# Where the first weights of a Strassen product begin in SBUF: 96 instead of 288 bytes behind a multiple of 512

## The chip, the cores and the metric

The kernel runs on one core of one Trainium2 chip. The metric is the device time of one execution in microseconds (us), as the median of the runs that were made; smaller is better. A profile is one further execution, recorded by the hardware profiler.

## What is computed

One residual block of a hybrid decoder over 512 positions of 1024 channels, in float32. Cut to its outline:

```
h = rmsnorm(x, norm1_g);  proj = h @ w_in
y_a = a_b * causal_dwconv(a_c * a_x)
y_b = native sparse attention (compressed, selected and windowed keys), 8 heads of 64
x = x + (sigmoid(gA) * (y_a @ w_a_out) + sigmoid(gB) * (y_b @ w_b_out)) @ w_o
h = rmsnorm(x, norm2_g);  gu = h @ w_ffn_in            # 1024 x 5632
g = causal_dwconv(gu[..., :2816], ffn_conv_w) + ffn_conv_b
x = x + (silu(g) * gu[..., 2816:]) @ w_ffn_out         # 2816 x 1024
```

The change lies in the product with `w_ffn_in`.

## The kernel before

Every float32 operand of a matmul is cut into a high part (rounded to the matmul's format) and a low part (the rest), and a product is three matmuls: high weights by high stream, high by low, low by high. The weights of a matmul are a 128x128 block (512 bytes in each partition) and the stream is what is multiplied by them, 512 or 256 columns wide.

The program has one queue of instructions per engine, whose order a scheduler fixed when the program was built. TensorE (PE) is busy from the first matmul to the last. The second half, from about 364 us, is the feed-forward part. `ff_strassen` goes over the 22 blocks of 128 hidden channels in 11 pairs, each once for the gate (n = 0) and once for the up weights (n = 1), so there are 22 calls of `ff_pair`. Each multiplies a 2x2 arrangement of weight blocks by a 2x2 arrangement of the stream with seven products in place of eight (Strassen's scheme in Winograd's form). The order of the products in `ff_pair` is a22, a11, a12, 2, 3, 4, 1. Each is a `dense` call: four steps along the contraction, each with high weights on the high and on the low stream (L405, L406), and then four with the low weights (L408). That is 12 matmuls of 256 columns a product and 84 a call. Between two calls `down_part` puts the product with `w_ffn_out`: matmuls of 512 columns that write `pdn`. The first call is written in another order (L969 and L975).

The names in the profile:

- `xf_h`, `xf_l`: high and low parts of the stream of all seven products; `ah`, `al`: the stream of `down_part`.
- `th`, `tl`: high and low parts of the weight block a22, written in `ff_forms`; two buffers each.
- `wh_s`, `wl_s`: parts of a11 and a12. `sh`, `sl`: parts of the four sums of blocks, by the names 1 to 4. `wh_d`, `wl_d`: parts of the weights of `down_part`.
- `gap_x`, `gap_w`: tiles that nobody writes or reads; they only move what is allocated after them.

A pool hands out addresses in the order in which the names of its tiles appear first. The pool `pw` begins directly behind `xf_l`. Line 832 names `th` there ahead of the gap, and everything else of the pool comes behind it. So the start addresses in a partition are, with the remainder on division by 512 (in this text: the phase):

| tile | starts at byte | phase |
| --- | --- | --- |
| `xf_h`, `xf_l` | 37152, 65824 | 288 |
| `th` (two buffers) | 94496, 96544 | 288 |
| `tl` (two buffers) | 98784, 100832 | 480 |
| sums, `sh`, `sl`, `p1` | 102880 to 135648 | 480 |
| `wh_s`, `wl_s`, `wh_d`, `wl_d` | from 204768 | 480 |
| `ah`, `al` | from 138720 | 480 |

Steps inside these tiles are multiples of 512 bytes, so each block of weights and each stretch of stream has the phase of its tile.

Of the kernel before, what the change touches and what calls it, by code (L numbers as in the profile page):

```python
# [11 lines left out]
F32 = mybir.dt.float32  # L12
# [6 lines left out]
P = 128  # L19
# [63 lines left out]
def tile_block(ctx: ExitStack, tc: tile.TileContext, xT, pos, par, par2, w_tok, w_a3, w_gate, w_ao, w_bo, w_o,  # L83
# [12 lines left out]
    def const(shape, name, dt=F32, pool=sb):  # L96
        return pool.tile(shape, dt, name=name, tag=name)
# [731 lines left out]
    xf_h = const([P, 4, 7, TH], "xf_h", F32R, px)  # L829
    xf_l = const([P, 4, 7, TH], "xf_l", F32R, px)  # L830
    pw = ctx.enter_context(tc.tile_pool(name="pw", bufs=1, side="left"))
    pw.tile([P, D // 2], F32R, name="th_", tag="th", bufs=2)
    const([P, 48], "gap_w", F32, pw)

    def x_forms(k, v):
        nc.vector.tensor_sub(v[:, T1:T3 + 1], v[:, 1:4:2], v[:, 0:2])
# [273 lines left out]
```

## Time and profile before

| what | value |
| --- | --- |
| median of 3 runs | 715.76 us (715.33 to 716.61) |
| the profiled execution | 715.21 us |
| its span, first to last instruction | 713.5 us |
| granted TensorE clock | 1.000 |

The span leaves out what the execution needs ahead of its first and behind its last instruction, 1.7 us here. In the listing by time a row is a run of like matmuls: its start, how long it lasted (the recorded end of the last one, and these overlap), the engine, the line, and what is written from what. A matmul's own recorded length is longer than the step from its start to the next start, since matmuls follow one another before they end; the step is what costs time, and it is read from the starts.

### The profile page before, as it was taken

To read this page: it belongs to the slowest core of one execution; us is meant where nothing else is said; L and a number is where in the kernel's file an instruction comes from. 1 tells how busy PE (TensorE), PEld (TensorE's weight loads), DVE (VectorE), ACT (ScalarE), POOL (GpSimd) and SP (SyncE) were. 2 spreads that over 40 slices of the span, in tenths; PEclk is the share of its full clock that TensorE was granted. 3 is DMA by queue.
4 is the path that set the end of the run, shared out by engine and by line. 5 is a ranking of instruction groups with operands and counts; after the bars stand their busy time and mean duration, and the time that the engine had idled before them with its cause. 6 is when DMAs were issued, how large, how long until landed. Compare 5 with 4: busy or idle time off the path is not lost.

```text
span 713.5 us, 11375 instructions
## 1 busy us (share of the span) xinstructions
PE 708.3 (99%) x4285; PEld 633.5 (89%) x4285; DVE 534.8 (75%) x957; ACT 432.6 (61%) x722; POOL 182.4 (26%) x179
## 2 busy tenths in 40 slices
PE   9999999999999999999999999999999999999997
PEld 9999878888888888888889999899999999999986
DVE  6887886687566878365795899988787877878643
ACT  7535655977667776522676767666555765647440
POOL 4051422133433334433012220221211222111110
PEclk9999999999999999999999999999999999999999
DMA  7333687511121122336386797987978779785565
GB/s 274 97 95 119 172 181 162 135 60 59 60 69 51 60 76 73 118 128 197 94 197 137 174 236 196 226 209 183 213 183 211 175 185 206 185 198 105 123 142 149
DMA packets 41142, 105.47 MB, mean 148 GB/s; under 512 B 3968, under 2 KB 9216, under 8 KB 41088
## 3 DMA queue, kind: packets, MB, share of 16 engines
q1 hardware_dynamic: 26528, 70.41, 30.4%
q0 software_dynamic: 14272, 34.08, 27.6%
q8 instruction: 33, 0.54, 0.3%
q10 hardware_dynamic: 288, 0.26, 0.1%
q14 instruction: 21, 0.17, 0.1%
HBM read 102.64 MB, written 2.10 MB: 147 GB/s over the span
## 4 chain that ended last, share of the span: by engine, by line
PE 96%; DMA 2%; ACT 1%; issue 0%; DVE 0%; POOL 0%; ACTq 0%; POOLq 0%
PE p L406 9%; PE p L405 9%; PE p L408 9%; PE pdn L406 6%; PE pdn L405 6%; PE pdn L408 6%; PE pg L406 4%; PE pg L405 4%; PE pg L408 4%; PE pa L405 2%; PE pt L681 2%; PE pa L406 2%; PE pa L408 2%; PE po L405 2%; PE po L406 2%; PE po L408 2%
## 5 line engine op out<-in xcount | busy, mean ns | idle before, releaser
L406 PE MATMUL p<-xf_l,sh 128*128 128x256 f32 x336 | 80.6, 277 | 0.0
L405 PE MATMUL p<-xf_h,sh 128*128 128x256 f32 x336 | 80.5, 277 | 0.0
L153 ACT ACTIVATE sh<-s 128x1024 fp32r<-128x1024 f32 x44 | 46.2, 1057 | 38.2 <-PE p L406 24.7
L406 PE MATMUL pdn<-al,wh_d 128*128 128x512 f32 x176 | 68.8, 391 | 0.0
L405 PE MATMUL pdn<-ah,wh_d 128*128 128x512 f32 x176 | 68.5, 390 | 0.0
L405 PEld LDWEIGHTS p<-xf_h,sh 128*128 128x128 f32 x336 | 63.0, 188 | 0.1
L406 PEld LDWEIGHTS p<-xf_l,sh 128*128 128x128 f32 x336 | 63.0, 188 | 0.1
L161 POOL DMA_DIRECT2D wl_s<-in_w_ff_dram x22 | 19.5, 885 | 167.2 <-ACT wl_s L160 155.9
L154 DVE TENSOR_TENSOR sl<-s,sh 128x1024 fp32r<-128x1024 f32 x44 | 53.8, 1224 | 8.7 <-ACT sh L153 8.7
L159 ACT ACTIVATE wh_s<-wr_s 128x1024 fp32r<-128x1024 f32 x22 | 23.3, 1059 | 53.1 <-PE pdn L406 50.1
L408 PE MATMUL p<-xf_h,sl 128*128 128x256 f32 x336 | 51.5, 277 | 0.0
L136 POOL TENSOR_TENSOR wl_g<-wr_g,wh_g 128x1024 fp32r<-128x1024 f32 x16 | 38.4, 2401 | 50.7 <-ACT wh_g L134 25.4
L405 PE MATMUL pg<-xg_h,wh_g 128*128 128x512 f32 x128 | 50.7, 396 | 0.0
L406 PE MATMUL pg<-xg_l,wh_g 128*128 128x512 f32 x128 | 50.6, 395 | 0.0
L408 PE MATMUL pdn<-ah,wl_d 128*128 128x512 f32 x176 | 47.7, 389 | 0.0
L161 POOL DMA_DIRECT2D wl_d<-in_w_dn_dram x22 | 26.5, 1203 | 77.2 <-ACT wl_d L160 69.0
L1029 DVE TENSOR_TENSOR x<-x,pdn 128x512 f32<-128x512 f32 x48 | 33.0, 688 | 16.2 <-PE pdn L408 15.5
L408 PEld LDWEIGHTS p<-xf_h,sl 128*128 128x128 f32 x336 | 44.6, 188 | 0.2
L405 PE MATMUL p<-xf_h,wh_s 128*128 128x256 f32 x168 | 40.5, 276 | 0.0
L406 PE MATMUL p<-xf_l,wh_s 128*128 128x256 f32 x168 | 40.5, 276 | 0.0
L408 PEld LDWEIGHTS pdn<-ah,wl_d 128*128 128x128 f32 x176 | 33.0, 188 | 6.9
L406 PEld LDWEIGHTS pdn<-al,wh_d 128*128 128x128 f32 x176 | 33.0, 188 | 6.2
(359 smaller groups left out, 2123.1 us busy)
## 6 DMA issues: line engine op xcount, KB each, us to landing
wr_s<-in_w_ff_dram SPq DMA_DIRECT2D x44, 512.0 KB, 4.9
wl_s<-in_w_ff_dram POOLq DMA_DIRECT2D x22, 512.0 KB, 7.2
wr_d<-in_w_dn_dram SPq DMA_DIRECT2D x22, 512.0 KB, 7.0
wl_d<-in_w_dn_dram POOLq DMA_DIRECT2D x22, 512.0 KB, 8.2
wr_g<-in_w_gate_dram SPq DMA_DIRECT2D x16, 512.0 KB, 3.4
wr_a<-in_w_a_dram SPq DMA_DIRECT2D x12, 512.0 KB, 4.1
tl<-in_w_ff_dram POOLq DMA_DIRECT2D x22, 256.0 KB, 6.9
wl_a<-in_w_a_dram POOLq DMA_DIRECT2D x10, 512.0 KB, 7.9
```

What stands on the lines that cost most here:

```text
L136: e.tensor_sub(lo[:, 0:n], raw[:, 0:n], hi[:, 0:n].bitcast(F32))
L153: hi = nc.scalar.activation(h, v, AF.Copy)
L154: nc.vector.tensor_sub(l, v, h.bitcast(F32))
L159: nc.scalar.activation(h, raw, AF.Copy)
L161: nc.gpsimd.dma_start(l if dst is None else dst, src, accum_op=ALU.add)
L405: nc.tensor.matmul(acc, wh, xh, start=first and i == 0, stop=False)
L406: nc.tensor.matmul(acc, wh, xl, start=False, stop=False)
L408: nc.tensor.matmul(acc, wl, xh, start=False, stop=last and i == len(units) - 1)
L681: nc.tensor.transpose(pt[:, i * P:(i + 1) * P], e[:, i, (kt + k0) * P:(kt + k0 + 1) * P], ident)
L1029: nc.vector.tensor_add(xj, xj, acc)
```

## The change

Two lines: a new gap of 320 bytes ahead of `th`, and a gap of 384 in place of 192 bytes behind it.

```diff
     pw = ctx.enter_context(tc.tile_pool(name="pw", bufs=1, side="left"))
+
+    const([P, 80], "gap_v", F32, pw)
     pw.tile([P, D // 2], F32R, name="th_", tag="th", bufs=2)
-    const([P, 48], "gap_w", F32, pw)
+    const([P, 96], "gap_w", F32, pw)
```

The start of `th` moves by 320 bytes, to 94816 and 96864, phase 96. `tl`, the sums, `sh`, `sl` and `p1` move by 320 + 192 = 512 bytes and keep phase 480. All else stays where it was. Every engine has the same instructions with the same waits in the same order as before.

## The prediction

> **What bounds the kernel now.** I read the page first: the line of busy times, then the chain that ended last.
>
> ```profile
> span 713.5 us, 11375 instructions
> PE 708.3 (99%) x4285; PEld 633.5 (89%) x4285; DVE 534.8 (75%) x957; ACT 432.6 (61%) x722; POOL 182.4 (26%) x179
> PE 96%; DMA 2%; ACT 1%; issue 0%; DVE 0%; POOL 0%; ACTq 0%; POOLq 0%
> ```
>
> PE is busy for 99% of the span and makes up 96% of the chain. In the feed-forward part, where the change lies, it has no idle time at all:
>
> ```profile
> core 0: us, PE busy (x) PEld busy (x) DVE busy (x) ACT busy (x) POOL busy (x), PEclk, DMA share, GB/s
> 477.60:687.90 210.30, 210.30 (x1513) 196.92 (x1512) 161.45 (x224) 123.56 (x164) 39.83 (x40) 1.00 0.77 178
> ```
>
> So the end of the kernel is set by how fast PE gets through its queue, and since the same matmuls stand there after the change, the only thing that can move is the step from one matmul to the next. I therefore read the starts in the listing by time, and first those of one ordinary call of `ff_pair`, the ninth of 22, with which the last 14 begin.
>
> ```profile
> start us, us, engine line op out<-in xcount [idle before <-releaser]
> 477.10 0.61 PE L408 MATMUL pdn<-ah,wl_d 128*128 128x512 f32 x2
> 477.55 0.28 PE L405 MATMUL p<-xf_h,th 128*128 128x256 f32 x1
> 477.67 0.28 PE L406 MATMUL p<-xf_l,th 128*128 128x256 f32 x1
> ...
> 478.38 0.28 PE L406 MATMUL p<-xf_l,th 128*128 128x256 f32 x1
> 478.50 0.62 PE L408 MATMUL p<-xf_h,tl 128*128 128x256 f32 x4
> 478.96 0.28 PE L405 MATMUL p<-xf_h,wh_s 128*128 128x256 f32 x1
> ...
> 487.12 0.39 PE L405 MATMUL pdn<-ah,wh_d 128*128 128x512 f32 x1
> ```
>
> The eight matmuls with `th` take 478.50 - 477.55 = 0.95 us, a step of 118.8 ns. The 76 others of the call take 487.12 - 478.50 = 8.62 us, a step of 113.4 ns. Same shape, same stream; what differs is that `th` has phase 288 and all other weights 480. The groups show it for the whole kernel in the mean recorded length of one matmul (the number of ns behind the busy us), which is longer where the step is:
>
> ```profile
> L406 PE MATMUL p<-xf_l,th 128*128 128x256 f32 x84 | 21.1, 282 | 0.0
> L406 PE MATMUL p<-xf_l,sh 128*128 128x256 f32 x336 | 80.6, 277 | 0.0
> L408 PE MATMUL p<-xf_h,tl 128*128 128x256 f32 x84 | 13.1, 276 | 0.0
> ```
>
> The Trainium skill says otherwise: by its page "TensorE: Matmul & The Clock Gate", section "Step-by-step: what each phase is for", the array reads the stream and the weights through two independent ports, and loading weights takes no read bandwidth from the running matmul. By that, no start address could matter and the change would be worth 0 us. The 118.8 against 113.4 ns above do not agree with it, and I go by the trace.
>
> **A second pace, which matters more.** Not every call runs at 113.4. Here is the call before, in which the scheduler put a part of `down_part` between the seventh and the eighth matmul with `th`:
>
> ```profile
> 462.79 0.39 PE L408 MATMUL pdn<-ah,wl_d 128*128 128x512 f32 x1
> 463.02 0.28 PE L406 MATMUL p<-xf_l,th 128*128 128x256 f32 x1
> 463.14 0.63 PE L408 MATMUL p<-xf_h,tl 128*128 128x256 f32 x4
> ...
> 472.09 0.39 PE L405 MATMUL pdn<-ah,wh_d 128*128 128x512 f32 x1
> ```
>
> The 76 matmuls behind that single `th` take 472.09 - 463.14 = 8.95 us, a step of 117.8 ns, with the same tiles at the same phases as above. It stays so to the call's end. The same slow pace begins where `down_part` is followed by weights of phase 480 with no `th` between:
>
> ```profile
> 421.48 0.39 PE L405 MATMUL pdn<-ah,wh_d 128*128 128x512 f32 x1
> 421.71 0.28 PE L405 MATMUL p<-xf_h,sh 128*128 128x256 f32 x1
> ...
> 422.65 0.28 PE L405 MATMUL p<-xf_h,sh 128*128 128x256 f32 x1
> ```
>
> Eight in 0.94 us are 117.5 ns a step. I looked for exceptions, and found a short one, 0.90 us for eight or 112.5 ns a step:
>
> ```profile
> 426.65 0.39 PE L405 MATMUL pdn<-ah,wh_d 128*128 128x512 f32 x1
> 426.88 1.07 PE L408 MATMUL p<-xf_h,sl 128*128 128x256 f32 x8
> 427.78 0.39 PE L406 MATMUL pdn<-al,wh_d 128*128 128x512 f32 x1
> ```
>
> So matmuls of 256 columns with weights at 480 have two paces, 113.4 and 117.8 ns, each of which keeps itself up. Out of `down_part` PE mostly falls into the slow one, and a full run of eight `th` at phase 288 hands it on to the fast one in each of the 14 calls from 477.55 us on. The detour over phase 288 costs 8 x 5.4 ns = 0.04 us a call and saves 76 x 4.4 ns = 0.33 us. That is the thing to ask of the new phase: not only how fast `th` itself runs, but in which pace it leaves PE.
>
> **The change, part by part.** No instruction, DMA or wait is added, removed or moved, so nothing is queued behind anything new.
>
> (1) `tl`, the sums, `sh`, `sl` and `p1` move by 512 bytes. Consecutive blocks of one tile are 512 bytes apart already, and the 76 matmuls above step over both kinds at one pace. I take 0, and see no reason for either sign.
>
> (2) `th` by itself. `th` serves 8 matmuls in 22 calls, 176 in all (84 + 84 in the groups, 8 in the first call's own lines). No row shows weights at 96 under a stream at 288, so the step is bounded from both sides. Below: the 113.4 ns of phase 480, 176 x -5.4 ns = -0.95 us. Above: where a call follows the fast pace directly, `th` at 288 holds its slowest steady step,
>
> ```profile
> 416.42 0.28 PE L405 MATMUL p<-xf_h,th 128*128 128x256 f32 x1
> ...
> 417.38 0.62 PE L408 MATMUL p<-xf_h,tl 128*128 128x256 f32 x4
> ```
>
> 0.96 us for eight, 120 ns. Nothing excludes a phase that is worse than 288, so I let it go as far above 118.8 as 113.4 lies below, 124 ns: +0.95 us. I take a point in the better half, 116 ns, halfway between the two paces that rows show: 176 x -2.7 = -0.5 us.
>
> (3) What `th` leaves behind. If it still hands on the fast pace, 0. If not, the 76 matmuls of each call run at 117.8: 14 x 76 x 4.4 ns = 4.7 us for the calls from 477.55 us on. For the rest I read the mean lengths, of the call at 463.14 us, of the whole stretch from 395 to 480 us, and of the first call's own lines:
>
> ```profile
> L408 PE MATMUL p<-xf_h,sl 128*128 128x256 f32 x16 | 2.5, 280 | 0.0
> ...
> L406 PE MATMUL p<-xf_l,sh 128*128 128x256 f32 x103 | 24.8, 278 | 0.0
> ...
> L969 PE MATMUL p<-xf_h,sl 128*128 128x256 f32 x12 | 3.3, 280 | 0.0
> ```
>
> A length of 280 ns goes with the slow pace, and 276 with the fast one above. So about half of the six calls from 395 to 480 us are fast, another 3 x 0.33 = 1.0 us to lose. On the other side, calls that are slow now could turn fast: the one at 463.14 (0.33 us) and the first two (0.33 us each), together -1.0 us. No other engine can cover a slower PE, and none stands in the way of a faster one by more than a fraction of this: DVE is the next, with 161 of 210 us in the window above.
>
> The sum of the likeliest case: 715.21 us of the profiled execution, -0.5, +0 is 714.7. The median of the runs stands 0.55 us above the profiled execution, which makes **715.3 us** as a median.
>
> **The rivals.**
>
> *The new phase still hands on the fast pace (my forecast).* For it: 96 lies 192 bytes below the stream's 288, as 480 lies 192 above, so the new place is not the one of `th` before, at the stream's own phase, and not that of the others; a switch of phase remains between a22 and what follows, and such a switch is what comes ahead of each fast stretch from 477.55 us on. With 113.4 to 124 ns for `th` and 0.4 us for the spread of the runs it gives 714.4 to 717.1 us.
>
> *The fast pace is lost (slower).* The place is the step from the last `th` to the first `tl` in each call: `down_part` leaves PE in the slow pace, and if eight matmuls at phase 96 act like those at 480 (421.71 us) or like a single `th` (463.02 us), the following 76 stay slow. It decides as soon as more than about 4 of 22 calls behave so, 1.43 us at 0.33 us each. `th` would then run at 117.8 itself, -0.2 us. All told 715.76 + 4.7 to 5.7 - 0.2 = 720.3 to 721.3 us, about 721. For it: of the entries into the fast pace that I read, all but the short one at 426.88 us go through 288. Against it: nothing shows that 288 is the only phase that does this.
>
> *Faster.* `th` at 113.4 (-0.95) and the three slow calls turned fast (-1.0): 713.8 us. It needs both, since -0.95 alone stays within what a measurement can tell from no change.
>
> *The address does nothing*: `th` is then slow for a reason of its own and stays at 118.8, 715.8 us. Against it: `tl` lies in the same pool, multiplies the same stretch of stream and is fast. (This is the outcome that the page of the Trainium skill named above would give.)
>
> **How the numbers follow.** I give the forecast 0.47, the lost pace 0.39, faster 0.10, no effect of addresses 0.04. What tells the first from the second is not in the trace, hence the closeness; I lean to the first since a change of phase within the call is kept. The forecast's own range is 714.4 to 717.1. The range that should hold 8 in 10 must take in the second case, with the same 0.4 us for the spread: 714.4 to 721.7. A measurement of this kernel tells about 0.2%, 1.4 us, from no change; faster by more 0.10, within 0.51, slower by more 0.39.
>
> **What the profile after would show.** Step (2): the starts of the eight matmuls with `th`, 0.91 to 0.99 us for a run, and their mean length beside the 282 ns. Step (3): the 76 that follow, 8.62 us if the pace is handed on and 8.95 us if not, and the mean length of `sh` at 276 to 277 or at 280 ns. Step (1) is wrong if the 76 show a third pace. I would be wrong altogether if the calls mix, some fast and some slow, or if PE shows idle time that it has not now.

## The result, and the profile after

| | before | after |
| --- | --- | --- |
| median, 4 runs each on one chip | 716.02 us (715.33 to 716.61) | 720.38 us (719.93 to 720.63) |
| the profiled execution | 715.21 us | 720.63 us |
| its span | 713.5 us | 718.9 us |

The ratio is 1.0064, with a 95% interval from 1.0052 to 1.0077: the change makes the kernel slower by some 4.5 us. That is the second rival of the prediction, the lost pace, and not the likeliest case.

The page of the kernel after: its busy times, its chain, and three of its groups (count | busy us, mean ns of one | idle before).

```profile
span 718.9 us, 11375 instructions
PE 712.6 (99%) x4285; PEld 637.1 (89%) x4285; DVE 535.1 (74%) x957; ACT 432.6 (60%) x722; POOL 181.7 (25%) x179
PE 97%; DMA 2%; DVE 0%; ACT 0%; POOL 0%; ACTq 0%; issue 0%
L406 PE MATMUL p<-xf_l,sh 128*128 128x256 f32 x336 | 82.3, 279 | 0.0
L406 PE MATMUL p<-xf_l,th 128*128 128x256 f32 x84 | 20.9, 281 | 0.0
L408 PE MATMUL p<-xf_h,tl 128*128 128x256 f32 x84 | 13.4, 279 | 0.0
```

PE is as full as before, with the same number of instructions, and but for one short wait, shown below, nothing new waits. It is the matmuls that became longer: `sh` went from 277 to 279 ns and `tl` from 276 to 279. Of all weights only `th` has another phase, and `th` itself is unchanged (281 beside 282). Next, the starts in the listing by time of the kernel after, for the ninth call and the first row of the tenth.

```profile
477.21 1.08 PE L408 MATMUL pdn<-ah,wl_d 128*128 128x512 f32 x4
478.12 0.28 PE L405 MATMUL p<-xf_h,th 128*128 128x256 f32 x1
...
479.07 0.63 PE L408 MATMUL p<-xf_h,tl 128*128 128x256 f32 x4
...
488.03 0.39 PE L405 MATMUL pdn<-ah,wh_d 128*128 128x512 f32 x1
...
493.50 0.28 PE L405 MATMUL p<-xf_h,th 128*128 128x256 f32 x1
```

The eight matmuls with `th` take 479.07 - 478.12 = 0.95 us, as before. The 76 behind them take 488.03 - 479.07 = 8.96 us, a step of 117.9 ns, where they took 8.62 us. The pace that `th` hands on is the slow one now. The call lasts 493.50 - 478.12 = 15.38 us (15.373 from the unrounded starts, beside 15.027 before), and the 13 others behind it last the same: 14 x 0.346 = 4.84 us. The remaining 0.57 us of the profiled executions' difference is there when the ninth call begins (478.12 beside 477.55): 0.42 us of it already at the first matmul of the first call (364.34 beside 363.91), ahead of every matmul with `th`, and 0.15 us from the first eight calls. The 0.42 us is no effect of the change: in the traces of all kernels here, which do the same work up to that point, the first call begins between 363.62 and 364.81 us.

In these eight the new phase also brings gains. The third call of the kernel after, which `th` enters from matmuls of 256 columns at the fast pace (`sl` stands between two pieces of `th` here):

```profile
396.42 0.28 PE L405 MATMUL p<-xf_h,th 128*128 128x256 f32 x1
396.53 0.28 PE L406 MATMUL p<-xf_l,th 128*128 128x256 f32 x1
396.65 1.07 PE L408 MATMUL p<-xf_h,sl 128*128 128x256 f32 x8
397.55 0.28 PE L405 MATMUL p<-xf_h,th 128*128 128x256 f32 x1
```

Ten steps in 1.13 us: `th` at phase 96 runs at 113 ns when it comes out of the fast pace, where phase 288 cost it 120. And the fifth call, entered from matmuls of 256 columns at the slow pace:

```profile
416.28 0.63 PE L408 MATMUL p<-xf_h,sl 128*128 128x256 f32 x4
416.75 0.28 PE L405 MATMUL p<-xf_h,th 128*128 128x256 f32 x1
...
417.11 0.28 PE L406 MATMUL p<-xf_l,th 128*128 128x256 f32 x1
...
417.67 0.62 PE L408 MATMUL p<-xf_h,tl 128*128 128x256 f32 x4
418.13 0.28 PE L405 MATMUL p<-xf_h,wh_s 128*128 128x256 f32 x1
```

Three steps of 120 ns (0.36 us), then five of 112 (0.56 us), and it stays fast behind them: from there phase 96 turns the slow pace into the fast one. In the ninth call the same run of eight, behind `pdn`, did not. So the pace that a run of `th` leaves depends on its phase and on what it comes out of. Against these gains, the fourth and the sixth call lose. The fourth falls into the slow pace in its middle, at two long steps of 0.22 us, and its 76 matmuls take 9.00 us in place of 8.61:

```profile
410.67 1.22 DVE L154 TENSOR_TENSOR sl<-s,sh 128x1024 fp32r<-128x1024 f32 x1
...
411.61 0.28 PE L405 MATMUL p<-xf_h,sh 128*128 128x256 f32 x1
411.72 0.28 PE L406 MATMUL p<-xf_l,sh 128*128 128x256 f32 x1
411.94 0.74 PE L408 MATMUL p<-xf_h,sl 128*128 128x256 f32 x4
```

The first of these long steps is a wait for VectorE (DVE). The weights `sl` are written by the row at 410.67 us, which ends at 411.89, and the matmul that reads them first starts at 411.94. At the pace of the rows before it would have started at 411.83. The same place in the kernel before:

```profile
410.12 1.22 DVE L154 TENSOR_TENSOR sl<-s,sh 128x1024 fp32r<-128x1024 f32 x1
...
411.88 0.62 PE L408 MATMUL p<-xf_h,sl 128*128 128x256 f32 x4
```

There `sl` was ready at 411.34 us, half a microsecond before its use. The fourth call begins at the same time in both traces (406.84 and 406.85 us): PE had made up the 0.42 us by which this execution was late, and VectorE had not. Behind this wait of about 0.1 us PE is in the slow pace. The kernels with `th` at 96 and `tl` at 288, and with `th` at 352 (both below), pass this place with no wait and stay fast, so phase 96 alone does not bring this loss; the timing does. The sixth call, behind `pdn`, loses as the late ones do: 68 matmuls in 8.01 us in place of 7.71.

### The profile page after: what moved, and what is told of

The parts are those of the page before. It is cut to its first block, busy times and chain, and to the rows that moved or that the text cites. A ratio compares the mean times of both kernels' runs of the same rounds, so it can differ in the third digit from the quotient of the medians.

```text
span 718.9 us, 11375 instructions
## 1 busy us (share of the span) xinstructions
PE 712.6 (99%) x4285; PEld 637.1 (89%) x4285; DVE 535.1 (74%) x957; ACT 432.6 (60%) x722; POOL 181.7 (25%) x179
## 4 chain that ended last, share of the span: by engine, by line
PE 97%; DMA 2%; DVE 0%; ACT 0%; POOL 0%; ACTq 0%; issue 0%
PE p L408 10%; PE p L406 10%; PE p L405 10%; PE pdn L406 6%; PE pdn L405 6%; PE pdn L408 6%; PE pg L406 4%; PE pg L405 4%; PE pg L408 4%; PE pa L408 3%; PE pa L405 3%; PE pa L406 3%; PE pt L681 2%; PE po L405 2%; PE po L406 2%; PE po L408 2%
## 5 line engine op out<-in xcount | busy, mean ns | idle before, releaser
L406 PE MATMUL p<-xf_l,sh 128*128 128x256 f32 x336 | 82.3, 279 | 0.0
L405 PE MATMUL p<-xf_h,sh 128*128 128x256 f32 x336 | 82.3, 279 | 0.0
```

Of the source, the lines that this page charges most:

```text
L405: nc.tensor.matmul(acc, wh, xh, start=first and i == 0, stop=False)
L406: nc.tensor.matmul(acc, wh, xl, start=False, stop=False)
```

## The experiments

The theory at the start: out of `down_part` PE is in the slow pace, and it is `th`'s phase alone that decides whether the rest of the call gets the fast one. All runs of one group share a chip with runs of the kernel before, whose median was 715.45 us in the first group, 715.40 in the second, 715.34 in the third and 715.58 in the last, of 13 or 14 runs each. Where a time has no interval, it is from one run.

### Everything moved by 512 bytes but `th`

```diff
     pw.tile([P, D // 2], F32R, name="th_", tag="th", bufs=2)
-    const([P, 48], "gap_w", F32, pw)
+    const([P, 176], "gap_w", F32, pw)
```

`th` stays at 288, and `tl`, the sums, `sh`, `sl` and `p1` lie where the change puts them.

> th stays at phase 288 as before, and all tiles behind it move by 512 bytes as the change moves them. Theory 1 (the phase of th alone decides, by the pace that its run leaves behind): the time of before, 716.0 us within 0.7, th at about 118.7 ns a step, the 76 matmuls behind it at 113.4. Theory 2 (the move of the other tiles by 512 bytes is what costs): about 720.4 us and 117.8 ns for the 76.

Measured: 715.42 us, ratio 0.9998 (0.9988 to 1.0007), with a slow `th` and 76 fast matmuls a call as before. The move of the others by 512 bytes is worth nothing, so all of the loss comes from `th`.

### `th` at phase 480, like the other weights

```diff
+    const([P, 48], "gap_v", F32, pw)
     pw.tile([P, D // 2], F32R, name="th_", tag="th", bufs=2)
-    const([P, 48], "gap_w", F32, pw)
```

> th lies at phase 480 like all other weights; the other tiles lie as before. Theory 1 (without a run at another phase PE keeps the slow pace that it comes into behind the matmuls of 512 columns): th and the 76 behind it at 117.8 ns a step in the 14 calls from the ninth on, 720 to 721.5 us. Theory 2 (phase 96 itself is bad, 480 is as good for th as for the others): th and the 76 at 113.4, 176 x 5.4 ns less than before, about 715 us.

Measured: 721.31 us, ratio 1.0073 (1.0056 to 1.0089). Its ninth call:

```profile
478.25 0.28 PE L405 MATMUL p<-xf_h,th 128*128 128x256 f32 x1
...
479.19 0.63 PE L408 MATMUL p<-xf_h,tl 128*128 128x256 f32 x4
...
488.15 0.40 PE L405 MATMUL pdn<-ah,wh_d 128*128 128x512 f32 x1
```

0.94 us for `th` and 8.96 for the rest: without any detour all 84 matmuls run at 117.5 to 118 ns. It is the detour over 288 that makes the call fast, and 96 does as little for the late calls as no detour at all.

### The product a22 moved behind five others, addresses as before

```diff
-        product(b45[:, lo], "a22", T4)
         product(b1[:, lo], "a11", B11)
...
         sums(c2, b37, c1[:, 1])
+        product(b45[:, lo], "a22", T4)
         product(b45[:, hi], 1, T1)
```

> All addresses as before (th at 288); the product with a22 stands sixth of seven in each call but the first, in place of first. Theory 1: behind the matmuls of 512 columns the 60 matmuls ahead of a22 run at 117.8 ns, th at 118 to 120, and only the 16 behind th at 113.4: 60 x 4.4 ns = 0.26 us a call, 14 to 17 calls, 3.7 to 4.5 us more than before, 719.7 to 720.5 us. Theory 2 (what costs is the address of th, wherever the run stands): no change, 716 us.

Measured: 719.88 us, ratio 1.0059 (1.004 to 1.0078), its span 717.3 us. A late call:

```profile
523.46 0.28 PE L405 MATMUL p<-xf_h,wh_s 128*128 128x256 f32 x1
...
530.53 0.28 PE L405 MATMUL p<-xf_h,th 128*128 128x256 f32 x1
...
531.48 0.62 PE L408 MATMUL p<-xf_h,tl 128*128 128x256 f32 x4
...
533.30 0.39 PE L405 MATMUL pdn<-ah,wh_d 128*128 128x512 f32 x1
```

Sixty matmuls from `pdn` to `th` take 7.07 us, 117.8 ns each. `th` at 288 takes 0.95 us here too. The 16 behind it take 1.82 us by these rows, 113.8 ns, and 1.814 us from the unrounded starts, 113.4 ns. The products that run at 113.4 ns in the kernel before, behind the run of `th`, are slow here ahead of it, at the same addresses. So the pace is a state that PE carries on, and not a property of an address.

### The stream moved to 480 too

```diff
-    const([P, 80], "gap_x", F32, px)
+    const([P, 128], "gap_x", F32, px)
...
-    const([P, 48], "gap_w", F32, pw)
```

With the larger gap ahead of it `xf_h` and `xf_l` begin at phase 480, and so do `th` and all other weights.

> Stream and all weights, th too, at phase 480. If what makes th slow at 288 is that it has the stream's own phase, all 1848 matmuls of the 22 calls run at 118.7 to 120 ns: 1672 x 5.3 to 6.6 ns = 9 to 11 us more than before, 725 to 727 us. If phase 480 of the weights is good by itself, whatever the stream's: 113.4 to 117.8 ns, 715 to 721 us.

Measured: 725.04 us, ratio 1.0126 (1.011 to 1.0143). A late call:

```profile
527.13 0.28 PE L405 MATMUL p<-xf_h,th 128*128 128x256 f32 x1
...
528.09 0.64 PE L408 MATMUL p<-xf_h,tl 128*128 128x256 f32 x4
...
537.21 0.40 PE L405 MATMUL pdn<-ah,wh_d 128*128 128x512 f32 x1
```

9.12 us for the 76 are 120 ns each, and the eight `th` ahead of them, behind `pdn`, take 0.95 us from the unrounded starts, 119 ns each. Those are the paces that `th` at 288 has under a stream at 288, out of the fast pace and behind `pdn`: weights and stream at one phase are the slowest pair that these runs show, and here no matmul of the call escapes it. The weight loads are recorded too, on their own row (PEld), and they become longer with it, from 188 to 192 ns; first the kernel before, then this one:

```profile
L406 PEld LDWEIGHTS p<-xf_l,sh 128*128 128x128 f32 x336 | 63.0, 188 | 0.1
L406 PEld LDWEIGHTS p<-xf_l,sh 128*128 128x128 f32 x336 | 64.4, 192 | 0.1
```

### `th` at 96 as in the change, and `tl` at 288

```diff
+
+    const([P, 80], "gap_v", F32, pw)
     pw.tile([P, D // 2], F32R, name="th_", tag="th", bufs=2)
+    const([P, 48], "gap_t", F32, pw)
+    pw.tile([P, D // 2], F32R, name="tl_", tag="tl", bufs=2)
     const([P, 48], "gap_w", F32, pw)
```

> The changed kernel (th at 96), with tl, the next four matmuls of each call, at phase 288. Theory 1 (a run at the stream's own phase hands PE on to the fast pace): th at 118.9 as in the changed kernel, tl at 117 to 120, and the 72 behind tl at 113.4 in the 14 calls from the ninth on; 716 to 717 us, the loss undone. If four matmuls are too few for it: 720 to 721 us. Theory 2 (th at 96 spoils the call whatever follows): 720.4 us.

Measured: 715.53 us, ratio 1.000 (0.999 to 1.001). A late call:

```profile
522.17 0.29 PE L405 MATMUL p<-xf_h,th 128*128 128x256 f32 x1
...
523.12 0.64 PE L408 MATMUL p<-xf_h,tl 128*128 128x256 f32 x4
523.60 0.28 PE L405 MATMUL p<-xf_h,wh_s 128*128 128x256 f32 x1
...
531.76 0.39 PE L405 MATMUL pdn<-ah,wh_d 128*128 128x512 f32 x1
```

`th` leaves PE in the slow pace, as in the change. Four `tl` at 288 then take 0.48 us, 120 ns each, and the 72 behind them 8.16 us, 113.3 ns. Four matmuls at the stream's phase undo the whole loss of the change. This settles where it came from.

### Other phases for `th`: 160, 352 and 32

```diff
+    const([P, 96], "gap_v", F32, pw)
     pw.tile([P, D // 2], F32R, name="th_", tag="th", bufs=2)
-    const([P, 48], "gap_w", F32, pw)
+    const([P, 80], "gap_w", F32, pw)
```

That is 160. For 352 the two gaps are 16 and 32 floats, and for 32 they are 64 and 112; the rest keeps phase 480.

> th at 160, 128 bytes below the stream's phase. If only the stream's own phase (288) hands on the fast pace: the 76 at 117.8 ns, 720 to 721 us. If all phases that lie a multiple of 128 bytes from the stream's do (and 96, 480 are alike because they lie 64 off such a multiple): the 76 at 113.4, about 716 us.

> th at 352, 64 bytes above the stream's phase and a multiple of 128 from 480 and 96. Only 288 hands on, or classes of 128 bytes: both say slow, 720 to 721 us. If what matters is that th comes near the stream's phase at all, it hands on: 716 us.

> th at 32, 256 bytes from the stream's phase. Only 288: slow, 720 to 721 us. Classes of 128 or of 256 bytes: fast behind th, about 716 us.

Measured: 721.28 us at 160 and 720.08 us at 352, with 76 slow matmuls in each late call; 715.53 us at 32. A late call of the kernel with 32:

```profile
522.69 0.28 PE L405 MATMUL p<-xf_h,th 128*128 128x256 f32 x1
...
523.64 0.62 PE L408 MATMUL p<-xf_h,tl 128*128 128x256 f32 x4
...
532.26 0.39 PE L405 MATMUL pdn<-ah,wh_d 128*128 128x512 f32 x1
```

0.95 and 8.62 us, exactly as with 288. The view that 288 alone does it falls, and so does one of classes of 128 bytes (160 lies 128 below 288 and fails). In the two pairs tried, phases that differ by 256 behave alike: 32 like 288, and 352 like 96, with the same gains in the early calls. 160 has none of these: in its fourth call `th` takes 0.94 us out of 256-column matmuls in the slow pace, and the 76 behind it 8.95. Of the six phases tried for `th`, the two that are the stream's own up to 256 hand on the fast pace out of `down_part`, and 96, 160, 352 and 480 don't.

### The stream of `down_part` moved

`ah` and `al`, the stream of the 512-column matmuls, lie at phase 480 like their weights. The theory: it is these that bring the slow pace, because stream and weights have one phase there. Here `th` is at 480, as in the second experiment, so that no detour helps, and a gap moves `ah` and `al` to 288 (48 floats), 352 (32) or 416 (16).

```diff
+    const([P, 48], "gap_v", F32, pw)
     pw.tile([P, D // 2], F32R, name="th_", tag="th", bufs=2)
-    const([P, 48], "gap_w", F32, pw)
...
     a_tiles(0)
+    const([P, 48], "gap_a", F32, pf)
```

> th at 480 (as in e2), and the stream of the matmuls of 512 columns, ah and al, at phase 288 in place of 480. If the slow pace is handed on by matmuls of 512 columns whose stream and weights have one phase, this takes the cause away and every call starts in the fast pace: th and the 76 at 113.4, at least 176 x 5.4 ns = 0.95 us less than before, 713.5 to 715 us. If any matmuls of 512 columns hand on the slow pace: 720 to 721.5 us as in e2.

> The same with ah and al at 352, 128 bytes from the weights' phase. Cause as in e9: 713.5 to 715 us if this phase leaves PE in the fast pace, 720 to 721.5 us if not; it tells whether 288 is special.

> The same with ah and al at 416, 64 bytes from the weights' phase; the two outcomes as in e10.

Measured with 288: 715.78 us, ratio 1.0005 (0.9996 to 1.0015), where the same kernel with `ah` and `al` at 480 had the ratio 1.0073. The place in it:

```profile
520.13 0.39 PE L405 MATMUL pdn<-ah,wh_d 128*128 128x512 f32 x1
...
522.88 0.28 PE L405 MATMUL p<-xf_h,th 128*128 128x256 f32 x1
...
523.78 0.62 PE L408 MATMUL p<-xf_h,tl 128*128 128x256 f32 x4
...
532.40 0.39 PE L405 MATMUL pdn<-ah,wh_d 128*128 128x512 f32 x1
```

All 84 matmuls are fast with no detour, 0.90 and 8.62 us: out of these 512-column matmuls PE comes in the fast pace. The expected gain over the kernel before did not come, for two reasons that the trace shows. The 512-column matmuls step at 2.75 / 12 = 229 ns; in the trace before, twelve of them between 519.91 and 522.63 us step at 227 (over all 24 of a stretch it is 228.9 beside 227.7). And the calls from the second to the sixth are slow but for 40 matmuls of the fifth, behind `pdn`. With 352 and 416 the times were 723.62 and 724.96 us, with spans of 721.9 and 722.0. The place with 352:

```profile
522.85 0.39 PE L405 MATMUL pdn<-ah,wh_d 128*128 128x512 f32 x1
...
525.65 0.28 PE L405 MATMUL p<-xf_h,th 128*128 128x256 f32 x1
...
526.59 0.63 PE L408 MATMUL p<-xf_h,tl 128*128 128x256 f32 x4
...
535.54 0.40 PE L405 MATMUL pdn<-ah,wh_d 128*128 128x512 f32 x1
```

The 512-column matmuls step at 2.80 / 12 = 233 ns there (232.4 over all 24), and the 84 behind them are slow, 0.94 and 8.95 us. So the theory holds only in part: the phase of `down_part`'s stream does decide the pace that it hands on, but being unlike its weights is not enough. 288 does it, and 352 and 416 do not. 288 is also the phase of `xf`, so that at 288 the 512-column matmuls have the same two phases, of weights and of stream, as the 256-column ones behind them. Whether this likeness is what counts, or the distance to the weights, no run tells.

### Both together: `th` at 352 and `ah`, `al` at 288

```diff
+    const([P, 16], "gap_v", F32, pw)
     pw.tile([P, D // 2], F32R, name="th_", tag="th", bufs=2)
-    const([P, 48], "gap_w", F32, pw)
+    const([P, 32], "gap_w", F32, pw)
...
     a_tiles(0)
+    const([P, 48], "gap_a", F32, pf)
```

> `th` at 352 and the stream of `down_part` at 288, all else as before. Theory 1 (the 512-column matmuls at 288 hand on the fast pace, as in the run before last but two; and `th` at 352 keeps the fast pace at 113.4 ns and turns the slow one into it when 256-column matmuls come ahead): all 84 matmuls of the 14 late calls at 113.4, a call of 15.01 us; of the calls up to the sixth, those with `th` behind 256-column matmuls fast from `tl` on. Against the run with `th` at 480 and this stream (715.78 us) two to four early calls at 0.33 us each come back: 714.5 to 715.1 us, faster than before by 0.1%, hardly more than can be told. Theory 2 (out of the 512-column matmuls `th` at 352 takes on 118.9 ns whatever their phase, and leaves the slow pace): 76 at 117.8 in the late calls and `pdn` slower by 2 ns for each of 528, about 721 us.

Measured: 715.01 us in 11 runs, ratio 0.999 (0.9981 to 1.0). A late call:

```profile
522.66 0.28 PE L405 MATMUL p<-xf_h,th 128*128 128x256 f32 x1
...
523.58 0.62 PE L408 MATMUL p<-xf_h,tl 128*128 128x256 f32 x4
...
532.19 0.39 PE L405 MATMUL pdn<-ah,wh_d 128*128 128x512 f32 x1
```

0.92 us for `th` (115 ns a step, not quite the 113.4 expected) and 8.61 for the rest. The slower 512-column matmuls take back what `th` saves, and the call lasts 15.027 us, as before. The gain lies in the early calls: from the start of the first call to that of the ninth 112.78 us pass (364.81 to 477.59), 0.86 us less than the 113.64 before. This is the lowest of all versions, 0.1% below the kernel before, and its interval ends at no change.

## Why the prediction went wrong, point by point

**The bound** was read rightly. PE is busy for 99% in every trace, and the loss is made of steps between matmuls. One point was too simple: that no other engine stands in the way of a faster PE by more than a fraction of this. It rested on VectorE's share of busy time over a long window, and in the fourth call of the kernel after PE, having gained on VectorE, waited for its `sl` (411.94 us), which cost that call 0.38 us.

**Part (1), the move by 512 bytes: 0.** Right, measured alone at 0.9998.

**Part (2), `th` by itself: -0.5 us at 116 ns.** Mis-sized. Behind `down_part` `th` keeps its 118.8 ns; only in the early calls, entered from 256-column matmuls, does it fall to between 113 and 117. Summed from the starts of all 22 calls, `th` saves 0.2 us. That is the rival's figure, though not for its reason.

**Part (3), what `th` leaves behind: 0.** This is the step that failed. The mechanism had been set out rightly, two paces that keep themselves up and a run of `th` that hands on one of them; what failed is the choice between its outcomes. The reason for leaning to the forecast was that "a change of phase within the call is kept". The runs show that behind the 24 matmuls of `down_part` a change of phase is not what does it. `th` at 96, 160 and 352 changes phase ahead of `tl` just as 288 does, and all three leave PE in the slow pace: the 76 take 8.95 us, 117.8 ns each. What turns it there is a run at the phase of the stream, or 256 from it: `th` at 288 or 32, or `tl` at 288.

The argument on distances, 96 as far below the stream as 480 lies above it, fell as well. With the period of 256 bytes that 32 and 352 suggest, 96 lies 64 above the stream, and 480 lies 192 above it. Most of the evidence in the trace pointed to the rival: all fast stretches but a short one began behind a run at 288, the stream's own phase, and 480 was seen to fail. The forecast preferred the wider rule, any change of phase, for which no row spoke that did not speak for the narrower one as well.

**The rival "the fast pace is lost".** Right in place, price and size: the last `th` to the first `tl`, 4.7 to 5.7 us less 0.2, together 720.3 to 721.3 us; measured were 720.38 us, 4.4 us above the median of the kernel before, and, in the profiled execution, 4.84 us in the 14 late calls. The further 1.0 us that it could lose in the early calls did not come, because some of them gained; with the wait in the fourth call they lost 0.15 us in all.

**The rival "faster"** had a piece of truth: the second call, slow before, turned fast with `th` at 96, and `th` became faster in the third to the fifth. This was far outweighed.

**The rival "the address does nothing"** is refuted most plainly by the fourth experiment, 715.45 against 725.04 us with no instruction changed. The rule of the Trainium skill, page "TensorE: Matmul & The Clock Gate", section "Step-by-step: what each phase is for", that weight loads take nothing from the running matmul, would make all these kernels equal, as the prediction read it; the steps of 113.4, 117.8 and 120 ns do not agree with that.

**What stays open** is why there are two paces. The record of a weight load overlaps that of the matmul ahead of it, and a stable offset between the two would fit a pace that lasts until something shifts it. The starts are recorded to 1 ns: on average a load starts 3.3 ns behind the matmul ahead in the fast ninth call of the kernel before, and 2.5 ns in the slow one of the kernel after, and it lasts 188 ns in both. No view of the trace shows the reads themselves, so this is a conjecture. Open is also the short fast stretch at 426.88 us in the kernel before, behind two `pdn`. It stands in every kernel with the stream at 288, `ah` and `al` at 480 and the products in the old order, whatever the phase of `th` (0.91 us for eight), and is gone in the four with `ah` and `al` moved (0.94 us), so it hangs on the phase of these too; why two such matmuls leave the fast pace and 24 the slow one is not known.

## What to carry to other kernels

Where matmuls follow each other without idle time, read the step from start to start and not the busy share; if the same shape on the same tiles shows two steps, look for what ran ahead of it. Start addresses of weights and stream are then something to try like any other setting, and a few padding bytes must be judged by the calls behind them too, not only by the tile that they move. Where the engine that sets the time gains a little, it can run into another engine's result that comes just too late, which a share of busy time does not show. When only one setting has been seen to work, a property that sets it apart (here the stream's own phase) deserves more weight than a wider rule under which an untried one would work as well.

## What the runs showed of the hardware that was not expected

- The step of a 128x256 float32 matmul with its own weights takes three lasting values at the same granted clock, 113.4, 117.8 and 120 ns, by the start addresses of weights and stream and by what ran before. From the kernel before to the one with everything at 480 that is 9.6 us of 715.
- In the two pairs tried, phases 256 bytes apart act alike: 32 like 288, and 352 like 96.
- With weights and stream at one phase the weight loads too are longer, 192 in place of 188 ns (the fourth experiment).
- Behind a wait of about 0.1 us in the middle of a fast call PE went on in the slow pace (411.94 us in the kernel after, seen once).
- Four matmuls at 120 ns can be worth 72 at 113.3 in place of 117.8 (the fifth experiment).
- The 512-column matmuls have it too: 227.7 ns over a late stretch of 24 with `ah`, `al` at 480, 228.9 at 288 and 232.4 at 352, under weights at 480. The fastest for themselves is not the one that hands on the fast pace.
